# Loading the first layer's norm modulation by 2048-column rows, and 128-feature blocks for the first norm

## The chip, the cores and the metric

The kernel runs on one core of a Trainium2 chip. The metric is the device time of one launch in microseconds (us), lower is better. The engines are TensorE (PE; its weight loads are PEld), VectorE (DVE), ScalarE (ACT), GpSimd (POOL) and SyncE (SP), which here only issues DMAs. All arithmetic is float32.

## The reference

Two layers of a decoder trunk on x of 256 tokens by 1024 features. Each layer's two norms are modulated by a vector `mod` that is computed from a conditioning vector c.

```
c_act = silu(c)
for l in range(2):
    mod = c_act @ ada_w[l] + ada_b[l]          # (1, 6144): ada_w[l] is 1024 x 6144
    sh1, sc1, g1, sh2, sc2, g2 = split(mod, 6)
    h = rms_norm(x) * (1 + sc1) + sh1          # the first norm
    mix = mixing_sublayer(h, w_in[l], w_out[l], ...)   # h @ w_in[l] (1024 x 3584), attention, HGRN2
    x = x + g1 * mix
    h = rms_norm(x) * (1 + sc2) + sh2          # the second norm
    x = x + g2 * grouped_moe(h, w_router, w_gate[l], w_up[l], w_down[l])   # 16 experts, top 2
return rms_norm(x, final_norm)
```

## The kernel before, in words

**Weights.** Everything large streams from HBM in pieces of 1 MiB (a tile of 128 partitions by 2048 numbers) through a ring of slots. `Ring.specs` is the list of pieces in order of use; SP issues the next one (L97) when a slot is free, and `release` frees a slot once its matmuls are queued. The list begins with the eight pieces of ada_w that give sh1 and sc1 of layer 0 (blocks b = 0 to 3 of 512 columns, two pieces each), then w_in of layer 0 (HF, HQ, AQ, ..., with further ada_w pieces between), w_out, the experts of layer 0, and the same for layer 1. `spec8` cuts a block of 512 columns into two pieces by the view "(p j) f -> p j f": partition p holds rows 8p to 8p+7, four of them in a piece, in runs of 512 numbers (2 KB).

**Modulation of the first norm, layer 0** (`ada_cols`, called in `mixing`). For each block b, `ada_rows` multiplies the silu of c by the block: four matmuls side by side in 32-column strips of PE per piece (L323, output tile `at`), and DVE folds in the bias (L331, tile `acc`). `ada_col` turns the block of 512 results into columns by eight matmuls against a vector of ones (L358), which sum the four strips, and DVE copies 64 partitions of them into `mcol` (L360). `mcol[p, w, j]` holds shift (w = 0) and scale plus one (w = 1) of feature 8p + j.

**The first norm.** `mixing` scales x by 1/rms into `xh` (L435), transposes it by 16 PE transposes that each take every eighth feature, `xh[:, tt, j::8]` (L438), and ACT and DVE apply scale and shift in turns into `hx` (L483, L481). `hx[:, j, :]` then is the operand of the input projection: L492 for the blocks whose result has channels on partitions, L503 for those with tokens there. 1/rms comes from four squares on ACT (L409), a sum on DVE (L416) and two POOL instructions (L315, L316, the second a power). `lower_bounds` and `rope_tables` run in the same stretch: small parameters are transposed by PE (L271) from `prow`, and sine and cosine tables are made on ACT and DVE (`cosf`, L307) and copied by POOL (L516).

**Layer 1's modulation of the first norm** is made during the mixing of layer 0 (`ada_next`): DVE multiplies and adds the eight pieces (L346, tile `accn`), PE sums over partitions into one row (`row_to_col`, L364), ACT copies the row (L367), and a POOL DMA spreads it into columns of `mcol` (L368). The second norm's blocks go through `row_to_col` too.

**The order on an engine** is not that of the code: a scheduler of the build sorts the instructions of each engine by a simulated timeline. On the chip every engine then works through its own list in that order and waits at each instruction for what it needs. In the trace a float32 matmul shows as two MATMUL records, so four matmuls read x8.

Of the kernel before, what the change touches and what calls it, by code (L numbers as in the profile page):

```python
# [14 lines left out]
P = 128  # L15
# [107 lines left out]
def tile_trunk(ctx: ExitStack, tc: tile.TileContext, x, c, positions, w_in, w_out, attn_norm,  # L123
# [17 lines left out]

    def spec8(label, src):
        v = src.rearrange("(p j) f -> p j f", j=8)
        return [(label + (h,), 512, v[:, 4 * h:4 * h + 4, :]) for h in range(2)]
# [27 lines left out]
    for l in range(L):  # L172
        if l == 0:
            for b in range(4):
                add_ada(l, b)
        for b in (HF, HQ, AQ, AK, AV, HI, HG):
            ring.specs += spec8(("in", l, b), w_in[l, :, b * 512:(b + 1) * 512])
            for a in ADA_AFTER[b]:
                add_ada(l, a)
            if l + 1 < L:  # L180
                for a in COL_AFTER[b]:
                    add_ada(l + 1, a)
# [26 lines left out]
    early = lp.tile([P, 2048], F32, tag="s3", name="early")  # L209
    prow = early[0:32, 0:128]  # L210
    pcol = cp.tile([P, 24], F32, name="pcol")
    gp.memset(brow, 0.0)
# [10 lines left out]
    for i, w in enumerate((lb_params, attn_norm, hgrn_norm)):  # L223
        sy.dma_start(prow[8 * i:8 * i + 8, :], w.rearrange("l (g p) -> (l g) p", p=P))
    with nc.allow_non_contiguous_dma(reason="small parameter columns"):
        sy.dma_start(posi, positions[0].rearrange("(t p) -> p t", p=P))
# [42 lines left out]
    def lower_bounds():  # L269
        pst = psum("mm")  # L270
        pe.transpose(pst[:, 0:24], prow[0:24, :], ident[0:24, 0:24])  # L271
        ve.tensor_copy(pcol, pst[:, 0:24])
        tmp4, mx4 = early[:, 132:136], early[:, 136:140]
# [77 lines left out]

    def ada_col(b, acc, tag):
        pst = psum(tag)
        w, half = {0: 0, 1: 1, 3: 2, 4: 3}[b // 2], b % 2
        av = acc.rearrange("k (m e) -> k m e", e=8)
        hs = slice(64 * half, 64 * half + 64)
        for j in range(8):
            pe.matmul(pst[hs, j:j + 1], av[:, :, j], ones[:, 0:1], start=True, stop=True,  # L358
                      tile_position=(0, 64 * half))
        ve.tensor_copy(mcol[hs, w, :], pst[hs, 0:8])  # L360

    def row_to_col(acc, w, half, row):
# [5 lines left out]
        gp.dma_start(mcol[64 * half:64 * half + 64, w, :], row[0:1, :].rearrange("o (p j) -> o p j", j=8))  # L368

    def ada_cols(l):  # L370
        prev = None
        for b in range(4):
            acc = ada_rows(l, b, "at")
            if prev is not None:
                ada_col(*prev, "mm")
            prev = (b, acc)
        ada_col(*prev, "mm")

# [52 lines left out]
    def mixing(l, sp, carry, scaled):  # L431
        xh = mp.tile([P, 2, D], F32, tag="h", name=f"xh{l}")
        pss = [psum(t) for t in ("tr", "tr", "hg", "hg")]
        for tt in range(2):
            ve.tensor_scalar(xh[:, tt, :], X[:, tt, :], nrm[:, tt:tt + 1], None, op0=ALU.mult)  # L435
            for j in range(8):
                o = (j % 2) * 256 + tt * 128
                pe.transpose(pss[j // 2][:, o:o + 128], xh[:, tt, j::8], ident)  # L438
        if l == 0:
            rope_tables()  # L440
            lower_bounds()
            ada_cols(0)
        sh = [lp.tile([P, 2048], F32, tag=f"s{i}", name=f"s{i}_{l}") for i in range(SHARED)]
# [305 lines left out]
        def ada_next():  # L749
            for i, b in enumerate(ORDER):  # L750
                for a in COL_AFTER[b]:
                    while used[0] < 8 * i + 8:
                        yield
                    box = []
                    yield from ada_rows_ve(l + 1, a, box)
                    row_to_col(box[0], a // 2, a % 2, None)
                    yield
# [630 lines left out]
```

## Time and profile before

| | |
|---|---|
| Time, median of 3 runs | 918.64 us (917.01 to 919.52) |
| The profiled execution's own time | 916.64 us |
| Its span in the profile | 914.9 us |
| PE busy | 833.1 us (91%) |
| DVE, ACT, POOL busy | 358.1, 191.6, 93.3 us |
| DMA | 293.16 MB, mean 320 GB/s |

The table says how much each engine did in the whole, not where the time is lost. The span falls into mixing and experts of layer 0, and the same of layer 1; the changed lines run at the start of layer 0 (up to 40 us), here and there in the mixing of layer 0, and in the first norm of layer 1.

### The profile page before, as it was taken

The numbers are of one execution on the slowest core, as the hardware profiler recorded it, in microseconds if no ns is written. First come the engines' busy times: TensorE is split into PE (matmuls) and PEld (weight loads), VectorE is DVE, ScalarE is ACT, GpSimd is POOL, SyncE is SP. The second block draws the span as 40 slices with busy tenths as digits, with TensorE's granted clock in tenths as the row PEclk, the third lists the DMA queues.
The fourth block names the chain that finished last, engine by engine and source line by source line (L and its number), as shares of the span: only waits on it lengthen the run. The fifth ranks groups of instructions, "written<-read, shape, count | busy, mean of one in ns | idle before, by whom it ended". The sixth has DMA issues, their size and how long they took to land. (4 is left out here: it accounts for less than half of the span.)

```text
span 914.9 us, 11907 instructions
## 1 busy us (share of the span) xinstructions
PE 833.1 (91%) x4569; PEld 428.8 (47%) x4569; DVE 358.1 (39%) x814; ACT 191.6 (21%) x386; POOL 93.3 (10%) x123
## 2 busy tenths in 40 slices
PE   4899999999899998889968999999989999889995
PEld 1588744654543342233316896565444434234322
DVE  2335886353722150222223468861363133023013
ACT  2121232331611110010021222252152011001112
POOL 0211330022000000000101332011200000000001
PEclk9899999999999999999998999999999999999998
DMA  9996577668789899999997633689669989999992
GB/s 331 385 330 224 184 276 266 256 261 342 303 336 406 342 416 402 416 404 404 411 387 261 230 122 111 231 303 336 239 227 394 409 334 422 395 416 407 422 386 90
DMA packets 97971, 293.16 MB, mean 320 GB/s; under 512 B 5558, under 2 KB 7886, under 8 KB 81512
## 3 DMA queue, kind: packets, MB, share of 16 engines
q1 hardware_dynamic: 97368, 291.93, 84.2%
q8 instruction: 40, 0.66, 0.3%
q14 instruction: 35, 0.29, 0.1%
q10 hardware_dynamic: 144, 0.26, 0.1%
q0 software_dynamic: 384, 0.03, 0.0%
HBM read 291.13 MB, written 1.05 MB: 319 GB/s over the span
## 5 line engine op out<-in xcount | busy, mean ns | idle before, releaser
L1049 PE MATMUL mm<-w,hg 128*32 128x512 f32 (+1 forms) x736 | 156.4, 595 | 2.1 <-DMA w<-in_w_up_dram 1.5
L1049 PE MATMUL mm<-s,hg 128*32 128x512 f32 (+1 forms) x576 | 141.2, 595 | 5.0 <-DMA s<-in_w_up_dram 3.5
L1049 PE MATMUL hg<-w,aT 128*32 128x512 f32 (+3 forms) x408 | 97.5, 584 | 2.9 <-DMA w<-in_w_down_dram 1.6
L492 PE MATMUL mm<-hx,w 128*128 128x256 f32 x352 | 82.6, 390 | 0.9 <-ACT hx L483 0.9
L1049 PE MATMUL hg<-s,aT 128*32 128x512 f32 (+1 forms) x312 | 72.7, 615 | 3.7 <-ACT aT L1073 2.5
L1049 PEld LDWEIGHTS mm<-w,hg 128*32 128x32 f32 (+1 forms) x736 | 42.3, 115 | 70.8 <-issue 65.6
L1066 DVE TENSOR_TENSOR a<-a,mm 128x512 f32<-128x512 f32 x14 | 9.6, 688 | 164.1 <-PE mm L1049 164.1
L492 PEld LDWEIGHTS mm<-hx,w 128*128 128x128 f32 x352 | 67.2, 195 | 13.9 <-issue 3.1
L1049 PEld LDWEIGHTS mm<-s,hg 128*32 128x32 f32 (+1 forms) x576 | 38.2, 119 | 59.5 <-issue 47.9
L492 PE MATMUL tr<-hx,w 128*128 128x256 f32 x256 | 57.3, 380 | 0.0
L1084 DVE SCALAR_TENSOR_TENSOR u<-hg,cws,mod 128x512 f32<-128x512 f32 x27 | 20.3, 751 | 90.4 <-PE hg L1049 84.7
L346 DVE SCALAR_TENSOR_TENSOR accn<-w,cact,accn 128x512 f32<-128x512 f32 x64 | 51.9, 811 | 4.7 <-DMA w<-in_ada_w_dram 3.3
L492 PEld LDWEIGHTS tr<-hx,w 128*128 128x128 f32 x256 | 48.2, 190 | 9.3 <-issue 3.1
L323 PE MATMUL at<-w,cz 128*32 128x512 f32 x208 | 34.5, 723 | 19.3 <-DMA w<-in_ada_w_dram 9.9
L503 PE MATMUL mm<-w,hx 128*128 128x512 f32 x112 | 50.9, 597 | 0.2 <-ACT s L575 0.2
L1093 DVE TENSOR_TENSOR X<-X,at 128x512 f32<-128x512 f32 x54 | 35.0, 683 | 29.7 <-PE at L1092 29.5
L1049 PEld LDWEIGHTS hg<-w,aT 128*32 128x32 f32 (+1 forms) x408 | 27.0, 120 | 41.6 <-issue 33.6
L1092 PE MATMUL at<-yy,scat 128*128 128x512 f32 x104 | 34.9, 433 | 11.5 <-ACT yy L1085 11.5
L1085 ACT ACTIVATE yy<-u 128x512 fp32r<-128x512 f32 x26 | 16.4, 629 | 117.2 <-DVE u L1084 117.2
L1049 PE MATMUL mm<-QT,hg 128*32 128x512 f32 (+1 forms) x96 | 37.3, 594 | 2.8 <-DMA QT<-in_w_up_dram 2.8
L1092 PEld LDWEIGHTS at<-yy,scat 128*128 128x128 f32 x104 | 16.5, 188 | 38.7 <-ACT yy L1085 20.4
L503 PEld LDWEIGHTS mm<-w,hx 128*128 128x128 f32 x112 | 20.6, 190 | 24.6 <-issue 24.0
(302 smaller groups left out, 1078.1 us busy)
## 6 DMA issues: line engine op xcount, KB each, us to landing
w<-in_ada_w_dram SPq DMA_DIRECT2D x42, 1024.0 KB, 9.2
w<-in_w_gate_dram SPq DMA_DIRECT2D x38, 1024.0 KB, 13.7
w<-in_w_down_dram SPq DMA_DIRECT2D x38, 1024.0 KB, 11.8
s<-in_w_up_dram SPq DMA_DIRECT2D x31, 1024.0 KB, 18.6
w<-in_w_in_dram SPq DMA_DIRECT2D x26, 1024.0 KB, 8.9
s<-in_w_gate_dram SPq DMA_DIRECT2D x25, 1024.0 KB, 12.9
w<-in_w_up_dram SPq DMA_DIRECT2D x24, 1024.0 KB, 18.9
s<-in_w_down_dram SPq DMA_DIRECT2D x24, 1024.0 KB, 17.1
```

Of the source, the lines that this page charges most:

```text
L323: pe.matmul(ps[32 * t:32 * t + 32, :], cz[:, r * 4 + t, :], w[:, t, :], start=(r == 0), stop=(r == 1), tile_position=(0, 32 * t))
L346: ve.scalar_tensor_tensor(acc, w[:, t, :], cact[:, j:j + 1], acc, op0=ALU.mult, op1=ALU.add)
L492: pe.matmul(o, w[:, cc], hx[:, j, :], start=j == 0 and cg % 2 == 0, stop=j == 7 and cg % 2 == 1)
L503: pe.matmul(pss[tt], hx[:, j, tt * 128:(tt + 1) * 128], w, start=j == 0, stop=j == 7)
L1049: marks[0] = pe.matmul(ps[a:a + n, :], lhs[:, a:a + n], ws[i], start=first, stop=last, tile_position=(0, a) if n < 128 else None)
L1066: ve.tensor_tensor(a, a, pu, op=ALU.mult)
L1084: ve.scalar_tensor_tensor(u, ps, cws, modB[3][:, hf * 512:(hf + 1) * 512], op0=ALU.mult, op1=ALU.mult)
L1085: ac.activation(yy[:, 0, :], u, AF.Copy)
L1092: pe.matmul(ps, sc[:, tt * 128:(tt + 1) * 128], yy[:, i, :], start=(i == 0), stop=(i == 1))
L1093: ve.tensor_tensor(X[:, tt, ds_], X[:, tt, ds_], ps, op=ALU.add)
```

## The change

Layer 0's sh1 and sc1 are loaded as eight pieces of one row in eight: piece j holds, on partition p, row 8p + j with all 2048 columns in one run (8 KB). `ada_first` takes the pieces as they come, and the four matmuls of a piece now are the four column blocks, each in its own strip of PE, added up over the eight pieces in one PSUM tile. ACT copies that tile once (L363), four transposes turn it (L366), and one DVE instruction picks the four columns that hold results, adds the bias and writes all of `mcol` for w = 0, 1 (L368). The bias comes from a new small DMA of ada_b into `prow` (L225) and through the transpose that was there for other parameters, now of 40 rows. Feature j*128 + p stands on partition p now, so `xh` is transposed in blocks of 128 neighbouring features, and w_in is viewed as "(j p) f -> p j f" in both layers. Layer 1's blocks are summed and turned into columns by four matmuls with `accn` as the stationary operand (L374) and an ACT copy (L376), in place of the row and the POOL DMA.

```diff
-    def spec8(label, src):
-        v = src.rearrange("(p j) f -> p j f", j=8)
+    def spec8(label, src, perm="(p j) f -> p j f"):
+        v = src.rearrange(perm, j=8)
...
         if l == 0:
-            for b in range(4):
-                add_ada(l, b)
+            v = ada_w[l, :, 0:2048].rearrange("(p j) f -> p j f", j=8)
+            ring.specs += [(("ada4", j), 2048, v[:, j:j + 1, :]) for j in range(8)]
...
-            ring.specs += spec8(("in", l, b), w_in[l, :, b * 512:(b + 1) * 512])
+            ring.specs += spec8(("in", l, b), w_in[l, :, b * 512:(b + 1) * 512], "(j p) f -> p j f")
...
+    sy.dma_start(prow[24:40, :], ada_b[0, 0:2048].rearrange("(k p) -> k p", p=P))
...
-        pe.transpose(pst[:, 0:24], prow[0:24, :], ident[0:24, 0:24])
-        ve.tensor_copy(pcol, pst[:, 0:24])
+        pe.transpose(pst[:, 0:40], prow, ident[0:40, 0:40])
+        ve.tensor_copy(pcol, pst[:, 0:40])
+        ve.tensor_scalar(pcol[:, 32:40], pcol[:, 32:40], 1.0, None, op0=ALU.add)
...
+    def ada_first():
+        ps = psum("at")
         for j in range(8):
-            pe.matmul(pst[hs, j:j + 1], av[:, :, j], ones[:, 0:1], start=True, stop=True,
-                      tile_position=(0, 64 * half))
-        ve.tensor_copy(mcol[hs, w, :], pst[hs, 0:8])
+            key, w = ring.take(("ada4", j))
+            for b in range(4):
+                pe.matmul(ps[32 * b:32 * b + 32, :], cz[:, j, :], w[:, 0, b * 512:(b + 1) * 512], start=(j == 0),
+                          stop=(j == 7), tile_position=(0, 32 * b))
+            ring.release(key)
+        acc = mp.tile([P, 512], F32, tag="acc", name="acc4")
+        ac.activation(acc, ps, AF.Copy)
+        pst = psum("mm")
+        for c in range(4):
+            pe.transpose(pst[:, c * 128:(c + 1) * 128], acc[:, c * 128:(c + 1) * 128], ident)
+        cols = mcol.rearrange("p w j -> p (w j)")[:, 0:16].rearrange("p (b c) -> p c b", b=4)
+        ve.tensor_tensor(cols, pst.rearrange("p (c b e) -> p c b e", c=4, b=4)[:, :, :, 0],
+                         pcol[:, 24:40].rearrange("p (b c) -> p c b", b=4), op=ALU.add)
+
+    def ada_col(b, acc):
+        w, half = b // 2, b % 2
+        pst = psum("at")
+        for c in range(4):
+            pe.matmul(pst[:, c:c + 1], acc[:, c * 128:(c + 1) * 128], ones[:, 0:1], start=True, stop=True)
+        ac.activation(mcol[:, w, 4 * half:4 * half + 4], pst[:, 0:4], AF.Copy)
...
-                pe.transpose(pss[j // 2][:, o:o + 128], xh[:, tt, j::8], ident)
+                pe.transpose(pss[j // 2][:, o:o + 128], xh[:, tt, j * 128:(j + 1) * 128], ident)
...
-            ada_cols(0)
+            ada_first()
...
-                    row_to_col(box[0], a // 2, a % 2, None)
+                    ada_col(a, box[0])
```

**PE at the start of layer 0.** From the last transpose of the first half of the tokens on, before (`w_5`, `w_6`, `w_7` are the last three ada_w pieces, `w_8` the first of w_in, `at` the sums, `mm_278` and `mm_288` the columns of blocks 2 and 3):

```order
L438 MATMUL hg_149<-cs,xh_145 128x128 x2
L323 MATMUL at_238<-w_5_99,cz 32x512 x4
L438 MATMUL tr_146<-cs,xh_145 128x128 x2
L438 MATMUL tr_147<-cs,xh_145 128x128 x2
L438 MATMUL hg_148<-cs,xh_145 128x128 x2
L438 MATMUL hg_149<-cs,xh_145 128x128 x2
L323 MATMUL at_263<-w_6_101,cz 32x512 x4
L358 MATMUL mm_278<-cs,acc_2_251 64x1 x8
L323 MATMUL at_263<-w_7_103,cz 32x512 x4
L358 MATMUL mm_288<-cs,acc_3_276 64x1 x8
L492 MATMUL mm_320<-hx,w_8_201 128x256 x2
```

And now, from the matmuls of `w_5` on (`acc_249` is ACT's copy of the sums; of the transposes the four rows of the first half of the tokens are left out, which read like those of the second):

```order
L359 MATMUL at_198<-w_5_100,cz 32x512 x4
...
L445 MATMUL tr_147<-cs,xh_146 128x128 x2
L445 MATMUL tr_148<-cs,xh_146 128x128 x2
L445 MATMUL hg_149<-cs,xh_146 128x128 x2
L445 MATMUL hg_150<-cs,xh_146 128x128 x2
L359 MATMUL at_198<-w_6_102,cz 32x512 x4
L359 MATMUL at_198<-w_7_104,cz 32x512 x4
L366 MATMUL mm_251<-cs,acc_249 128x128 x4
L499 MATMUL mm_279<-hx,w_8_203 128x256 x2
```

The matmuls of `w_5` moved ahead of all transposes of `xh`, and the two groups of column matmuls gave way to one group of four transposes.

**POOL on the way to 1/rms.** Before (`nrm` is 1/rms, `s` the tile of the copied tables):

```order
L315 TENSOR_SCALAR nrm<-nrm 128x2
L516 COPY s_0_304<-sinf 128x256
L316 TENSOR_TENSOR nrm<-nrm,mhalf 128x2
L457 MEMSET s_0_299 64x4x256
L458 MEMSET s_0_299 64x4x256
L459 MEMSET QT 64x4x256
L460 MEMSET QT 64x4x256
L516 COPY s_0_304<-cosf 128x256
```

And now:

```order
L523 COPY s_0_263<-sinf 128x256
L317 ISA
L317 TENSOR_SCALAR nrm<-nrm 128x2
L523 COPY s_0_263<-cosf 128x256
L318 TENSOR_TENSOR nrm<-nrm,mhalf 128x2
L464 MEMSET s_0_258 64x4x256
```

The copy of the cosine table, which stood behind the power and four memsets, now stands ahead of the power that ends `nrm`.

**DVE in the mixing of layer 0**, where the first pieces for layer 1 (`accn`) meet the start of HGRN2 (`hg` its PSUM tiles). Before:

```order
L346 SCALAR_TENSOR_TENSOR accn_0_551<-w_18_364,cact,accn_0_551 128x512 x4
L346 SCALAR_TENSOR_TENSOR accn_0_551<-w_19_372,cact,accn_0_551 128x512 x3
L595 TENSOR_TENSOR s_0_300<-s_0_298,s_0_299 64x1024 x2
L346 SCALAR_TENSOR_TENSOR accn_0_551<-w_19_372,cact,accn_0_551 128x512
L606 TENSOR_TENSOR s_0_299<-s_0_299,s_0_298 64x4x128 x2
L602 TENSOR_TENSOR s_0_301<-cs,hg_443 128x8x128
```

And now:

```order
L348 SCALAR_TENSOR_TENSOR accn_0_510<-w_18_323,cact,accn_0_510 128x512 x4
L602 TENSOR_TENSOR s_0_259<-s_0_257,s_0_258 64x1024 x2
L348 SCALAR_TENSOR_TENSOR accn_0_510<-w_19_331,cact,accn_0_510 128x512
L613 TENSOR_TENSOR s_0_258<-s_0_258,s_0_257 64x4x128 x2
L348 SCALAR_TENSOR_TENSOR accn_0_510<-w_19_331,cact,accn_0_510 128x512 x3
L609 TENSOR_TENSOR s_0_260<-cs,hg_402 128x8x128
```

Three of the `accn` instructions moved from ahead of the start of HGRN2 to between its second and third step.

## Rows read from the trace of the kernel before

**Rows 1.** The page's DMA share in 40 slices of the span, in tenths

```profile
DMA  9996577668789899999997633689669989999992
```

**Rows 2.** PE's groups by line, 39.8 to 230 us: xcount | busy us, mean ns | idle before <-releasers

```profile
L492 PE MATMUL mm<-hx,w 128*128 128x256 f32 x192 | 46.3, 396 | 0.9 <-ACT hx L483 0.9
...
L618 PE MATMUL hg<-s,s 128*128 128x128 f32 x112 | 14.2, 276 | 1.0 <-DVE s L631 1.0
...
L503 PE MATMUL mm<-s,hx 128*128 128x512 f32 x16 | 7.1, 599 | 1.2 <-DMA s<-in_w_in_dram 1.2
...
L364 PE MATMUL at<-accn,cs 128*1 128x512 f32 x8 | 4.1, 590 | 0.0
...
L683 PE MATMUL at<-s,QT 128*128 128x128 f32 x16 | 3.6, 305 | 0.8 <-DVE mx L689 0.8
...
L600 PE MATMUL hg<-heads,s 128*128 128x2 f32 x16 | 1.8, 246 | 0.0
```

**Rows 3.** Timeline, x to xh: start us, us, engine, line, tiles [idle before <-releaser]

```profile
18.39 0.63 ACT L409 ACTIVATE junk<-X 128x512 f32<-128x512 f32 x1 [15.82 <-DMA X<-in_x_dram]
...
24.39 0.40 POOL L516 COPY s<-sinf 128x256 f32<-128x256 f32 x1 [1.00 <-ACT sinf L304]
...
24.75 0.70 POOL L316 TENSOR_TENSOR nrm<-nrm,mhalf 128x2 f32<-128x2 f32 x1
...
24.95 0.18 DVE L307 TENSOR_SCALAR cosf<-early 128x64 f32<-128x64 f32 x1
...
25.92 2.54 DVE L435 TENSOR_SCALAR xh<-X,nrm 128x1024 f32<-128x1024 f32 x2
```

**Rows 4.** Timeline, from xh to the first matmul of the input projection

```profile
27.07 1.12 PE L438 MATMUL tr<-cs,xh 128*128 128x128 f32 x4 [0.92 <-DVE xh L435]
...
28.97 1.94 PE L323 MATMUL at<-w,cz 128*32 128x512 f32 x8
...
30.84 0.71 PE L438 MATMUL tr<-cs,xh 128*128 128x128 f32 x4
...
31.93 1.07 PE L323 MATMUL at<-w,cz 128*32 128x512 f32 x8
...
32.93 2.08 PE L358 MATMUL mm<-cs,acc 128*64 128x1 f32 x16
...
34.94 1.06 PE L323 MATMUL at<-w,cz 128*32 128x512 f32 x8
...
36.07 0.75 DVE L331 SCALAR_TENSOR_TENSOR acc<-brow,cs,at 128x512 f32<-128x512 f32 x1 [0.87 <-PE at L323]
...
36.87 2.08 PE L358 MATMUL mm<-cs,acc 128*64 128x1 f32 x16 [0.87 <-DVE acc L331]
...
39.81 6.96 PE L492 MATMUL mm<-hx,w 128*128 128x256 f32 x20 [0.86 <-ACT hx L483]
```

**Rows 5.** Windows: stretch, us, busy us of PE, PEld, DVE, ACT, POOL, PEclk, DMA, GB/s

```profile
31.00:37.80 6.80, 5.93 (x48) 4.05 (x48) 1.63 (x3) 0.00 (x0) 0.00 (x0) 1.00 1.04 384
37.90:44.60 6.70, 5.84 (x20) 4.79 (x21) 2.08 (x5) 1.94 (x4) 0.00 (x0) 0.50 1.05 386
44.70:55.00 10.30, 10.30 (x51) 9.09 (x50) 0.00 (x0) 1.88 (x2) 0.00 (x0) 1.00 1.05 387
...
358.70:362.10 3.40, 1.86 (x13) 0.73 (x11) 0.69 (x1) 0.60 (x1) 0.00 (x0) 1.00 1.05 387
```

**Rows 6.** DMA packets of 40 to 56 us, and of 340 to 350 us

```profile
DMA packets 3111, 6.18 MB, mean 386 GB/s; under 512 B 95, under 2 KB 95, under 8 KB 3111
...
DMA packets 583, 4.25 MB, mean 425 GB/s; under 512 B 64, under 2 KB 64, under 8 KB 64
```

**Rows 7.** DMA issues of 18.3 to 18.6 us: size, us to landing

```profile
w<-in_ada_w_dram SPq DMA_DIRECT2D x1, 1024.0 KB, 10.9
```

**Rows 8.** Timeline: an ACT copy of a whole PSUM tile

```profile
64.83 0.60 ACT L400 ACTIVATE mod<-at 128x512 f32<-128x512 f32 x1 [7.49 <-PE at L399]
```

**Rows 9.** DMA share in 40 slices of 212 to 230 us

```profile
DMA  9999999999998930000077989999989999999999
```

More of the change, by code (lines that the diff above doesn't have):

```diff
@@ L209, in tile_trunk @@
     early = lp.tile([P, 2048], F32, tag="s3", name="early")
-    prow = early[0:32, 0:128]
-    pcol = cp.tile([P, 24], F32, name="pcol")
+    prow = early[0:40, 0:128]
+    pcol = cp.tile([P, 40], F32, name="pcol")
     gp.memset(brow, 0.0)
@@ L350, in ada_rows_ve @@
         out.append(acc)
[L352 to L356, printed above, removed]
-        for j in range(8):
-            pe.matmul(pst[hs, j:j + 1], av[:, :, j], ones[:, 0:1], start=True, stop=True,
-                      tile_position=(0, 64 * half))
-        ve.tensor_copy(mcol[hs, w, :], pst[hs, 0:8])
+    def ada_first():
+        ps = psum("at")
+        for j in range(8):
+            key, w = ring.take(("ada4", j))
[17 more added lines that the diff above has]
+        ac.activation(mcol[:, w, 4 * half:4 * half + 4], pst[:, 0:4], AF.Copy)
     def row_to_col(acc, w, half, row):
@@ L368, in row_to_col @@
         gp.dma_start(mcol[64 * half:64 * half + 64, w, :], row[0:1, :].rearrange("o (p j) -> o p j", j=8))
[L370 to L377, printed above, removed]
     def ada_block(l, b, route):
```

## Prediction

> **What bounds the kernel now.** The page comes first, and of it the DMA share by slices [rows 1]: it is full up to about 70 us, falls to 6 to 9 tenths up to 200 us, and is full through most of the experts. So the start might be bound by the loads, the mixing hardly, the experts partly. The groups of PE's matmuls in the mixing of layer 0 tell the second thing [rows 2]: over 190 us PE sat idle 0.9 + 1.0 + 1.2 + 0.8, that is 3.9 us, and every other group has nothing before it. From the first matmul of the input projection (39.81 us) to the end of the mixing PE is the bound, and whatever brings that first matmul forward brings the experts forward.
>
> What holds it back until 39.81 is read from two pieces of the timeline. The first [rows 3]: x lands at 18.39, ACT squares it, the scheduler has put table loads, sine and cosine between, and POOL's power ends at 25.45; DVE starts to scale x at 25.92. The second [rows 4]: from 27.07 PE works through transposes, the pieces of ada_w and the column matmuls one after another. Its idle time there is the 0.87 us for DVE's bias and the 0.86 us for the copy and the first piece of `hx`. The last piece of ada_w lands 10.9 us after its issue at about 18.4 [rows 7], at 29.3, but is multiplied at 34.94. It is PE's queue, not the load, that is late.
>
> The third thing is PE's clock [rows 5]: 1.00 (2.4 GHz) from 31.0 to 37.8, 0.50 (1.2 GHz) from 37.9 to 44.6, 1.00 again from 44.7. It had risen after PE had worked without a pause from 27.07; it fell after a stretch in which PE did one full group (1.06 us), column matmuls and two waits. So the projection ran its first 4.8 us at half speed and lost 2.4 us.
>
> **The change part by part.** Start of PE's work on `xh`. Runs of 8 KB move faster than runs of 2 KB: 425 against 386 GB/s [rows 6], for 1 MiB 2.47 against 2.72 us. Four pieces stand ahead of x, so x lands 1.0 us earlier. The ends: nothing gained if what tells the two windows apart is not the run length, 1.0 us if it is; I take the gain, since the windows differ in little else. Against it, POOL now copies the cosine table ahead of the power. The table is ready at 25.13 on the old clock, the copy takes 0.40 and the power 0.70, so `nrm` is done at about 26.3 in place of 25.45, plus 0.9. Net zero on `nrm`; DVE's other small work, which kept `xh` until 25.92, is shorter by two bias and two column instructions less one new, so `xh` starts 0.5 us earlier, and the transposes at 26.6. If the loads are no faster they start at 27.5.
>
> PE from there. Transposes of the first half 1.9 us, of the second 1.9 (still at the lower clock; at the upper 1.1): 30.4. The matmuls of `w_5`, 1.94 us between the two halves before, now run in the idle time ahead, since `w_5` lands by 24 (two pieces of 2.7 ahead of the last, at 29.3) and no transposes are ready. `w_6` and `w_7` at the upper clock, 1.07 + 1.06: 32.5. That takes for granted that 3.8 us of work without a pause raise the clock as before. Nothing says that the moment of the rise repeats to the microsecond; half a microsecond goes on top for it: 33.0.
>
> The tail. Before, from the end of `w_7` (36.0): bias on DVE, 2.08 us of column matmuls, copy, first `hx`, 39.81, in all 3.8 us. Now: ACT copies the tile, 0.60 [rows 8] and 0.1 to start; four transposes, which as eight records cost half of the sixteen of `xh`, 1.2 us; DVE's addition of 16 numbers a partition, 0.2 as the small DVE instructions of this stretch (0.18 in [rows 3]), and 0.1; then as before 0.86 less the copy's 0.2, 0.65. In all 2.85 us: the first matmul of the projection at 35.8 in place of 39.81, **4.0 us earlier**. By parts: 0.5 for `xh`, 1.9 for `w_5`, 2.0 for the columns of block 2, 1.0 for the tail, less about 0.9 because the second transposes run at the lower clock, and 0.5 for the rise.
>
> The clock after that. Between the end of `w_7` and the projection PE now has 2.85 us with 1.2 us of transposes in it, where it had 3.8 us with column matmuls of one moving column. It is followed by the projection without a gap. From 358.7 to 362.1 PE stood idle for 1.5 us between full matmuls, and the clock was 1.00 [rows 5]. I take it that the clock stays up: **2.4 us**. The ends are 0 (it falls as before) and 2.4; a fall that starts with the projection and lasts as long as the whole of the old one, 6.8 us, costs 3.4 and so 1.0 more than before.
>
> Layer 1's columns. Four times, two records of 0.59 us, in all 0.95 to 1.0 (8 records of L364 in 4.1 us) [rows 2], become eight with a full weight load and one moving column. The nearest is L600, 16 records in 1.8 us, 0.9 for eight. Zero, at most 0.3 each if the loads don't overlap; I add 0.2. The four POOL DMAs and the row copies that go were hidden under PE's work.
>
> At nothing: the transposes of neighbouring features (the same records; a reading order is not seen in any row), the 40-row transpose, the one DVE instruction and the one small DMA, hidden in waits of the first 18 us on x. The new view of w_in has the same 2 KB runs, farther apart; its first piece landed at some 33 (0.44 MiB of constants and itself, 3.9 us, behind the last of ada_w), 6 us before its use, which comes 4 us earlier. Uncovered, 10% more for a load costs 0.3 us a piece.
>
> Sum: 4.0 + 2.4 - 0.2 = 6.2 us. From the profiled execution's 916.64 that gives 910.4; the median of the runs is 2.0 above that execution, so 912.4 on the scale of the runs. The experts of layer 0 run partly at the pace of DMA, but their stream starts from PE's work: at 218 to 222 us the DMA engines stand still [rows 9], because slots, not the stream, were the limit. So the shift should reach the end.
>
> **The rivals.** *The clock falls again.* For it: it did so in nearly the same place, and PE waits twice. Against it: the waits are shorter and the matmuls between fuller. Then 4.0 - 1.0 - 0.2 = 2.8 earlier, or 4.0 if it loses no more than before: 914.6 to 915.8.
>
> *Transposes don't wake the clock.* If only the matmuls of pieces count, PE runs at the lower clock through `w_6` and `w_7` (3.9 us: 34.3), the tail adds 2.85 (37.2), and the clock falls once more for 6.8 us: 2.6 - 1.0 - 0.2 = 1.4 earlier, 917.2. The Trainium skill, TensorE: Matmul & The Clock Gate, Part 4, states that PE's transpose mode does not count as busy for the clock. By that rule this rival is the forecast; the trace speaks more against it than for it, since the clock rose at 31.0 after a stretch that was half transposes [rows 4, 5].
>
> *The loads get slower.* Each ada_w run now is 8 KB at a distance of 192 KiB from the next partition's; before, the same partition's runs followed at 24 KiB. If that took 30% more time per piece, 0.8 us, the last one would land at 29.3 + 8 x 0.8 = 35.7, and the projection start at 35.7 + 1.1 + 2.85 = 39.6: no gain, 918.4. Against it: the 8 KB runs of the experts are the fastest in the trace. The Trainium skill, DMA: Bandwidth & Descriptors, Latency and other measured facts, gives a fall from 207 to 164 GB/s where rows lie 2 MiB apart in place of 512 KiB; 192 KiB is below both, and no run here shows such a distance with 8 KB runs.
>
> *Slower: HGRN2's start is late on DVE.* Three `accn` instructions now stand between its second and third step. The third step feeds PE's L618 and, at the end of that chain, frees the slots for the last w_in pieces, for which PE already waits 1.2 us [rows 2]. Three instructions of 0.8 us are 2.4 us. Since the chain alternates between PE and DVE, a PE list that was sorted for a faster one could stall at several places. From 6.2 us of such stalls on it decides; at 9 the time is 921.4. Against it: PE's idle for DVE is 1.8 us in the whole mixing.
>
> **How the numbers follow.** The forecast (clock stays, 910.5 to 914.5) 0.53; the clock falls again 0.2; transposes don't count 0.08; slower loads, or a gain swallowed by the experts' stream, 0.11; slower 0.08. A measurement of this kernel can tell some 0.3%, 2.8 us. Faster takes the forecast, and of the second case all that is over 2.8, with its share: 0.53 + 0.2 + the better half of the third, 0.77; same 0.15; slower 0.08. The range of 8 in 10 leaves out the slower case and the top of the slow loads above, and a little below: 910.0 to 917.3. The likeliest's own is 910.5 to 914.5.
>
> **What would show it.** The first L499 between 35 and 36.5 us; `w_5` multiplied before the transposes; the x wait ending near 17.4; PEclk 1.00 through 37 to 45 us, and no more than 4.5 us of PE idle from there to the end of the mixing. It is wrong where the first L499 comes after 38, where PEclk shows 0.50 for the projection's start, or where PE waits for `hg` or `s` by more than 3 us in the mixing.

## The result and the profile after

The changed kernel takes 906.03 us (median of 4 runs, 905.32 to 907.78) where the kernel before takes 918.77 (4 runs, 917.01 to 919.52): ratio 0.9869, 95% interval 0.9855 to 0.9883, so 12.7 us faster where 6.2 were forecast. The profiled execution of after is the longest of its four, 907.78 us with a span of 905.9; that of before, 916.64 us, lies below all four of its timed runs. Between the two profiles the gain is therefore only 8.9 us.

The timeline of after from x to `xh` answers to [rows 3]; columns as there.

```profile
17.43 0.63 ACT L416 ACTIVATE junk<-X 128x512 f32<-128x512 f32 x1 [14.86 <-DMA X<-in_x_dram]
...
23.42 0.39 POOL L523 COPY s<-sinf 128x256 f32<-128x256 f32 x1 [21.64 <-ACT sinf L306]
23.91 0.19 POOL L317 TENSOR_SCALAR nrm<-nrm 128x2 f32<-128x2 f32 x1
24.21 0.40 POOL L523 COPY s<-cosf 128x256 f32<-128x256 f32 x1
24.57 0.70 POOL L318 TENSOR_TENSOR nrm<-nrm,mhalf 128x2 f32<-128x2 f32 x1
...
25.31 2.96 DVE L442 TENSOR_SCALAR xh<-X,nrm 128x1024 f32<-128x1024 f32 x2 [1.09 <-POOL nrm L318]
```

x comes 0.96 us earlier (17.43 for 18.39). POOL's cosine copy stands ahead of the power, as the order said, and takes back part of that; `xh` starts 0.61 us earlier.

The same view from `xh` to the projection, on PE, ACT and DVE, answers to [rows 4].

```profile
22.51 1.93 PE L359 MATMUL at<-w,cz 128*32 128x512 f32 x8 [0.52 <-DMA w<-in_ada_w_dram]
...
26.89 1.11 PE L445 MATMUL tr<-cs,xh 128*128 128x128 f32 x4 [2.45 <-DVE xh L442]
...
29.50 0.91 PE L445 MATMUL hg<-cs,xh 128*128 128x128 f32 x4
30.34 1.92 PE L359 MATMUL at<-w,cz 128*32 128x512 f32 x16
...
32.33 0.60 ACT L363 ACTIVATE acc<-at 128x512 f32<-128x512 f32 x1 [8.83 <-PE at L359]
32.98 0.66 PE L366 MATMUL mm<-cs,acc 128*128 128x128 f32 x4 [0.72 <-ACT acc L363]
33.68 0.18 DVE L368 TENSOR_TENSOR mcol<-mm,pcol 128x16 f32<-128x16 f32 x1 [5.41 <-PE mm L366]
33.90 1.02 ACT L490 ACTIVATE hx<-tr,mcol 128x256 f32<-128x256 f32 x2 [0.97 <-DVE mcol L368]
34.51 0.70 PE L499 MATMUL mm<-hx,w 128*128 128x256 f32 x2 [0.87 <-ACT hx L490]
```

`w_5` is multiplied at 22.51, ahead of the transposes; these run without a pause, `w_6` and `w_7` follow as one group, and the projection starts at 34.51 in place of 39.81. The windows with the granted clock answer to [rows 5].

```profile
26.90:30.10 3.20, 3.20 (x15) 3.20 (x16) 1.37 (x1) 0.00 (x0) 3.09 (x3) 0.50 0.98 339
30.20:31.00 0.80, 0.80 (x10) 0.29 (x12) 0.00 (x0) 0.00 (x0) 0.00 (x0) 1.00 1.05 407
31.00:37.80 6.80, 5.21 (x31) 3.48 (x24) 2.09 (x5) 2.52 (x5) 0.00 (x0) 1.00 1.05 409
37.90:44.60 6.70, 6.70 (x35) 5.90 (x34) 0.00 (x0) 1.88 (x2) 0.00 (x0) 1.00 1.05 405
```

The clock stays at 1.00 through the projection's start, where before it was 0.50 from 37.9 to 44.6. Then one thing that no step spoke of: the last column, 405 to 409 GB/s where before showed 384 to 387. The DMA lines of after for 40 to 56 us (against [rows 6]) and for the experts, 250 to 450 us:

```profile
DMA packets 3287, 6.54 MB, mean 408 GB/s; under 512 B 96, under 2 KB 96, under 8 KB 3287
...
DMA packets 21741, 81.63 MB, mean 408 GB/s; under 512 B 1248, under 2 KB 1248, under 8 KB 15299
```

In 40 to 56 us the sizes are as before (nearly all 2 KB), the engines are as full, yet 3287 packets pass for 3111. In the experts the kernel before has this line:

```profile
DMA packets 19903, 77.99 MB, mean 390 GB/s; under 512 B 1176, under 2 KB 1176, under 8 KB 13464
```

The step from 390 to 408 is not all due to the packets. The experts of layer 0 begin at 247.59 us in before and at 240.12 in after, so the window holds another part of them. The changed kernel with its slots at another place (`after_unpad`, below), whose experts begin at 239.28, moves 400 GB/s in the same window:

```profile
DMA packets 20984, 79.90 MB, mean 400 GB/s; under 512 B 1213, under 2 KB 1213, under 8 KB 14582
```

So more than half of the step goes with where the window falls, and 8 of the 18 GB/s are left for the packets. Their records in the trace show it directly: in the first 60 us a 2 KB packet takes a median of 84 ns, before 87; in the experts an 8 KB packet 309, before 312.

The stages in one table, from one profile each; every border is the start of a group on PE (first projection matmul, first router transpose of X, first expert matmul), worked out from the instruction records. The kernels of the rows from `before_pad` on come below.

| | start | mixing 0 | router 0 | experts 0 | mixing 1 | router 1 | experts 1 | span |
|---|---|---|---|---|---|---|---|---|
| before | 39.81 | 190.29 | 17.49 | 242.57 | 172.49 | 16.04 | 236.16 | 914.85 |
| after | 34.51 | 188.12 | 17.49 | 241.19 | 172.48 | 16.04 | 236.08 | 905.91 |
| before_pad | 39.19 | 189.86 | 17.49 | 241.97 | 172.49 | 16.02 | 233.68 | 910.69 |
| after_256 | 34.62 | 188.04 | 17.51 | 241.62 | 172.48 | 16.04 | 233.91 | 904.21 |
| l1row | 35.46 | 188.06 | 16.10 | 241.12 | 172.47 | 16.05 | 235.58 | 904.83 |
| after_unpad | 35.58 | 187.66 | 16.03 | 244.23 | 172.48 | 16.03 | 237.09 | 909.11 |
| after_128 | 35.42 | 187.87 | 16.03 | 244.16 | 172.49 | 16.04 | 236.27 | 908.28 |
| before_warm | 40.20 | 189.39 | 17.50 | 242.83 | 172.48 | 16.05 | 238.49 | 916.94 |
| xfirst | 32.03 | 190.59 | 16.04 | 236.12 | 171.52 | 16.04 | 235.37 | 897.72 |
| xfirst_warm | 35.29 | 188.18 | 16.03 | 239.89 | 172.49 | 17.50 | 234.11 | 903.49 |

A router stage is 16.0 or 17.5, as the clock does or does not fall there; this differs between executions of one kernel (router 1 of before takes 16.04 here and 17.49 in two more profiles of it). It and the experts' stage move single spans by a few us, so sizes below are taken from ratios of medians, and the table only says where. Each ratio is to runs of the kernel before on the same chip; the experiments ran on several chips, so their medians alone don't compare to a microsecond.

### The profile page after: what moved, and what is told of

It reads as the page before. It is cut to its first block, busy times and chain, and to the rows that moved or that the text cites. A ratio compares the mean times of both kernels' runs of the same rounds, so it can differ in the third digit from the quotient of the medians.

```text
span 905.9 us, 11822 instructions
## 1 busy us (share of the span) xinstructions
PE 824.9 (91%) x4533; PEld 423.6 (47%) x4533; DVE 354.0 (39%) x808; ACT 190.4 (21%) x387; POOL 91.1 (10%) x119
## 5 line engine op out<-in xcount | busy, mean ns | idle before, releaser
L499 PE MATMUL mm<-hx,w 128*128 128x256 f32 x352 | 80.3, 382 | 0.9 <-ACT hx L490 0.9
L1056 PEld LDWEIGHTS hg<-w,aT 128*32 128x32 f32 (+1 forms) x408 | 26.2, 120 | 43.8 <-issue 35.8
L1099 PE MATMUL at<-yy,scat 128*128 128x512 f32 x104 | 35.0, 434 | 11.5 <-ACT yy L1092 11.5
L1099 PEld LDWEIGHTS at<-yy,scat 128*128 128x128 f32 x104 | 16.5, 188 | 38.8 <-ACT yy L1092 20.5
L638 DVE TENSOR_TENSOR s<-s,s 64x256 f32<-64x256 f32 x56 | 31.5, 562 | 0.7
```

The costliest lines, as they stand in the source:

```text
L499: pe.matmul(o, w[:, cc], hx[:, j, :], start=j == 0 and cg % 2 == 0, stop=j == 7 and cg % 2 == 1)
L638: ve.tensor_tensor(qv[:, :, :, 1, :], qv[:, :, :, 1, :], tv[p0:p1, :, :, 0:1].to_broadcast([p1 - p0, 4, nb, h]), op=ALU.mult)
L1056: marks[0] = pe.matmul(ps[a:a + n, :], lhs[:, a:a + n], ws[i], start=first, stop=last, tile_position=(0, a) if n < 128 else None)
L1099: pe.matmul(ps, sc[:, tt * 128:(tt + 1) * 128], yy[:, i, :], start=(i == 0), stop=(i == 1))
```

## The experiments

The theories after the first comparison. One: the change's own steps (earlier start, clock kept) gave it all, and the faster packets are one execution's luck or come of the 8 KB runs. Two: `pcol` grew by 16 columns of 4 bytes, and with it every tile allocated behind it, the slots of all the large loads, moved by 64 bytes; packets are faster for where they land.

**Is the packet time one execution's?** `before_b1` and `before_b2` are the kernel before again, `after_a1` the changed kernel, no line changed.

> The kernel before once more, to see how far its executions differ and where. Theory A (the 8.9 us between the two profiles are the change, the remaining 3.8 us between the medians are scatter of single executions): time 917 to 920, first matmul of the projection between 39 and 41.5 us, its length from there to the experts' end within 1 us of the profile before, and what is over it lies in the stretches where the clock is low or in the experts. Rival B (the profile before was an outlier at its start): first matmul of the projection at 42 us or later, 2 us or more behind the profile before.

> The same kernel, a third profile. Theory A: as in the run ahead of it, 917 to 920, the first matmul of the projection at 39 to 41.5. Rival B: at 42 or later.

> The changed kernel once more. Theory A (all of the gain is made ahead of the end of the first projected block: the earlier first matmul, 5.3 us, and the clock that stays up, 2.4 us; what is over 7.7 us is scatter): ratio to before 0.986 to 0.991, first matmul of the projection at 34 to 35.5 us, clock 1.00 through the first 10 us of it. Theory B (part of the gain is made in the experts of layer 0, whose loads meet free slots earlier): the experts of layer 0 take 241.2 us again, 1.4 less than in the profile before and than in the two other profiles of before.

Measured: 919.10 and 919.75 us, one time each; `after_a1` 908.43 (6 runs), ratio 0.9876 (0.9856 to 0.9897). The start is at 39.78 and 40.44 in before, at 34.21 in after; mixing 0 takes 190.5 and 190.2 against 187.8. So the first profile of before was no outlier at its start. Theory B is borne out too: the experts of layer 0 take 241.48 us in `after_a1`, against 243.01 and 243.25. The first copy of before moves 386 GB/s at 40 to 50 us, as the first profile did:

```profile
DMA packets 1945, 3.86 MB, mean 386 GB/s; under 512 B 62, under 2 KB 62, under 8 KB 1945
```

The packet time belongs to the program: the median of 2 KB packets in the first 60 us is 86 to 87 ns in all three profiles of before and 84 in both of after.

**Is it the 8 KB runs?** `runs2k` keeps the changed kernel, but loads each of the first eight pieces as two DMAs with 2 KB runs.

```diff
-            self.parts.append([(v[:, :, a:b], src[:, :, a:b]) for a, b in cuts])
+            if label[0] == "ada4":
+                q = "p o (x y f) -> p (o y) x f"
+                dv, sv = v.rearrange(q, x=2, y=2), src.rearrange(q, x=2, y=2)
+                self.parts.append([(dv[:, y], sv[:, y]) for y in range(2)])
+            else:
+                self.parts.append([(v[:, :, a:b], src[:, :, a:b]) for a, b in cuts])
```

> The changed kernel with each of the first eight pieces loaded by two DMAs whose runs are 2 KB in place of 8 KB; nothing else differs. If the longer runs brought x forward by 1.0 us and that goes through to the projection: x is used at 18.3 in place of 17.4, the projection starts at 35.3 to 35.6, and the time is 0.8 to 1.2 us more than the changed kernel's (ratio to before 0.987 to 0.989). If the run length is hidden behind the small instructions on ACT, POOL and DVE: the projection starts at 34.5 and the time is the changed kernel's.

Measured: 908.26 us (5 runs), ratio 0.9871 (0.9851 to 0.9891), no difference from the changed kernel. x is used at 18.13 and the projection starts at 35.67, where PE waits 1.56 us for the first piece of w_in. So the long runs bring x 0.7 us forward (18.13 to 17.43), but the 0.8 to 1.2 us that were expected at the end do not show. At 40 to 50 us it still moves 407 GB/s: the later loads' speed does not come of the runs.

**Is it the place?** Three kernels change nothing but the room that `pcol` takes. `before_pad` gives the kernel before the changed kernel's room; `after_unpad` and `after_128` move the changed kernel's slots to other places.

```diff
 before_pad
-    pcol = cp.tile([P, 24], F32, name="pcol")
+    pcol = cp.tile([P, 40], F32, name="pcol")[:, 0:24]
 after_unpad
-    pcol = cp.tile([P, 40], F32, name="pcol")
+    pcol = cp.tile([P, 88], F32, name="pcol")[:, 0:40]
 after_128
-    pcol = cp.tile([P, 40], F32, name="pcol")
+    pcol = cp.tile([P, 72], F32, name="pcol")[:, 0:40]
```

> The kernel before with nothing but a longer tile: pcol takes 40 columns in place of 24 as in the change, which moves every tile behind it by 64 bytes a partition, the ring's slots from 64 past a multiple of 128 bytes to a multiple of 512. No instruction differs. Theory C (the place of the slots sets the time of a DMA packet, and through it 1.5 to 3 us of the change's gain): packets of 2 KB take 84 ns in the median from 20 to 55 us in place of 88, the experts of layer 0 take 241.3 us in place of 242.6 to 243.3, and the time is 2 to 3.5 us less than before's. Rival D (the packets are faster for another reason: which rows a piece holds, the view of w_in): packets stay at 88 ns and the time is before's within 0.5 us.

> The changed kernel with pcol at 88 columns: the slots stand 64 bytes past a multiple of 128 again, as before the change; no instruction differs. Theory C: packets of 2 KB take 88 ns, of 8 KB 315; the experts of layer 0 take 242.5 to 243.5 us; the time is 1.5 to 3.5 us more than the changed kernel's 908.4 (ratio to before 0.989 to 0.991). Rival D: 84 and 310 ns, and the changed kernel's time.

> The changed kernel with pcol at 72 columns: slots at a multiple of 128 bytes, but not of 256 or 512. Theory C with a step of 128 bytes or less: packets of 84 ns and the changed kernel's time. If it takes a multiple of 256 or 512: 88 ns, and the time of the run with the slots 64 bytes off.

Later `after_256` (a room of 104 columns) was added, to tell which multiple it takes.

> The changed kernel, pcol's room 104 columns in place of 40, so that every tile behind it starts 256 bytes past a multiple of 512 (in the changed kernel on a multiple of 512, in the kernel before 448 past it); no instruction differs. If a multiple of 256 bytes is enough for a load's destination: packets of 2 KB 84 ns, time 906 +- 1.5, as the changed kernel. If it takes a multiple of 512: 88 ns and 910 to 911, as with the room of 88 and of 72 columns. If the place of the tiles is not the cause at all, nothing ties the packets to the room, and 88 or 84 may come here with any time.

The DMA lines at 40 to 50 us, first `before_pad`:

```profile
DMA packets 2056, 4.08 MB, mean 408 GB/s; under 512 B 64, under 2 KB 64, under 8 KB 2056
...
q1 hardware_dynamic: 2056, 4.08, 105.0%
```

then `after_unpad`:

```profile
DMA packets 1950, 3.86 MB, mean 386 GB/s; under 512 B 63, under 2 KB 63, under 8 KB 1950
...
q1 hardware_dynamic: 1950, 3.86, 104.9%
```

The engines are equally busy in both (last figure, share of 16 engines), and the packets that pass differ by 5%. With the bytes by which the slots' start lies past a multiple of 512, from the addresses of the built programs:

| kernel | bytes past 512 | GB/s at 40 to 50 us | median, us | ratio (interval) |
|---|---|---|---|---|
| before | 448 | 386 | 918.65 | 1 |
| before_pad | 0 | 408 | 914.81 | 0.9960 (0.9944 to 0.9976) |
| after | 0 | 409 | 906.03 | 0.9869 (0.9855 to 0.9883) |
| after_256 | 256 | 408 | 905.74 | 0.9868 (0.9849 to 0.9887) |
| after_unpad | 192 | 386 | 910.90 | 0.9909 (0.9893 to 0.9925) |
| after_128 | 128 | 387 | 910.07 | 0.9924 (0.9897 to 0.9950) |

No instruction differs between before and `before_pad`, nor among the four kernels with the change. The place moves both kernels by 0.4 to 0.55%, 3.7 to 5 us, and of the places tried the two on a multiple of 256 bytes (0 and 256) are fast; 128, 192 and 448 are not. The Trainium skill, DMA: Bandwidth & Descriptors, How a descriptor splits into AXI transactions, says that the first transaction of a descriptor which doesn't start on a multiple of 256 bytes starts at the boundary below it, and that the bytes fetched ahead of the start are unused and still cost beats, the 32-byte steps of the transfer. These runs agree in where the border lies; the page puts it for the reading side of a transfer, and here it is the place that is written. That this is the mechanism here is not shown.

Not every number came as expected. `before_pad` gains 3.8 us between the medians, where 2 to 3.5 were expected; the experts of layer 0 take 241.97 there in place of 241.3, and 244.2 in `after_unpad` and `after_128` in place of 242.5 to 243.5. For the changed kernel the table of stages says where the place costs: `l1row` (below; slots as in after) and `after_unpad` start within 0.12 us of each other and both keep the clock up in router 0, and the experts of layer 0 then take 241.12 and 244.23, three microseconds more at the worse place. For the kernel before the profiles do not tell where: `before_pad` is shorter mainly in the experts of layer 1 (233.68 for 236.16), but after and `after_256`, both at a good place, differ there by as much.

**Layer 1's columns.** `l1row` takes them back to the row matmul with DMAs on POOL's queue.

```diff
+    def row_to_cols(b, acc):
+        w, half = b // 2, b % 2
+        ps = psum("at")
+        pe.matmul(ps[0:1, :], ones[:, 0:1], acc, start=True, stop=True)
+        row = mp.tile([P, 512], F32, tag="acc", name="row")
+        ac.activation(row[0:1, :], ps[0:1, :], AF.Copy)
+        for j in range(4):
+            gp.dma_start(mcol[:, w, 4 * half + j:4 * half + j + 1],
+                         row[0:1, 128 * j:128 * j + 128].rearrange("o (p e) -> o p e", e=1))
...
-                    ada_col(a, box[0])
+                    row_to_cols(a, box[0])
```

> The changed kernel with layer 1's blocks summed into a row by one matmul again and spread by POOL DMAs (four a block, of single numbers, since the layout is the new one). The prediction's term: 0.2 us to the better, hidden otherwise, so the time is that of the changed kernel within 0.5 us. Rival: the rows on ACT and the DMAs that POOL waits for held the mixing up; then the mixing of layer 0 takes 1 us or more over the 188 of the changed kernel.

Measured: 906.80 us (4 runs), ratio 0.9869 (0.9851 to 0.9887), that of the change. The group in the mixing of layer 0 is, in after,

```profile
L375 PE MATMUL at<-cs,accn 128*128 128x1 f32 x32 | 3.9, 243 | 0.0
```

against 4.1 us before [rows 2]. This part is worth nothing that can be measured, either way (the interval is 1.7 us to either side).

**The clock alone.** `before_warm` is the kernel before with matmuls that nobody reads: two of 128x256 in the wait for the last bias, two in that for the last column copy.

```diff
+            if (l, b, r) == (0, 3, 1):
+                warm = psum(tag)
+                for n in range(2):
+                    pe.matmul(warm[:, 0:256], w[:, 0, 0:128], w[:, n, 0:256], start=True, stop=True)
             ring.release(key)
...
+        warm = psum("at")
+        for n in range(2):
+            pe.matmul(warm[:, 0:256], acc[:, 0:128], acc[:, 0:256], start=True, stop=True)
```

> The kernel before with four matmuls of 128x256 whose result nobody reads, two in the wait for the last bias and two in the wait for the last column copy, just ahead of the projection; nothing else differs. If the fall of the clock there cost 2.4 us and came of PE's thin work: granted clock 1.00 from 31 to 45 us, first matmul of the projection at 39.8 to 40.3, mixing 187.7 to 188.2 in place of 190.3, 916 to 917 (ratio 0.9975). If the clock falls anyway at that time, or costs nothing: 918 to 919.5 (ratio 1.000).

Its PE row at that place, and its windows:

```profile
35.17 1.07 PE L323 MATMUL at<-w,cz 128*32 128x512 f32 x8
36.16 1.13 PE L328 MATMUL at<-w 128*128 128x256 f32 x4
37.22 2.08 PE L362 MATMUL mm<-cs,acc 128*64 128x1 f32 x16
39.23 1.13 PE L384 MATMUL at<-acc 128*128 128x256 f32 x4
40.20 2.17 PE L499 MATMUL mm<-hx,w 128*128 128x256 f32 x9
```

```profile
31.00:37.80 6.80, 6.80 (x53) 4.54 (x49) 1.65 (x3) 0.00 (x0) 0.00 (x1) 1.00 1.05 386
37.90:44.60 6.70, 6.70 (x37) 5.92 (x37) 2.08 (x5) 1.94 (x4) 0.00 (x0) 1.00 1.05 387
...
157.20:160.60 3.40, 3.18 (x4) 1.51 (x5) 0.39 (x2) 0.59 (x1) 0.52 (x1) 0.50 1.05 406
```

Measured: 915.92 us (12 runs, 914.02 to 920.29), ratio 0.9982 (0.9967 to 0.9998): 1.7 us (0.2 to 3.0). The pauses are filled and the clock doesn't fall at 37.9; the projection starts 0.4 us later and still the kernel gains. Mixing 0 took 189.39 in the profiled execution, not the 187.7 to 188.2 expected: the clock fell once within it, in 157.2 to 160.6 us, which before did not show. By an estimate half of those 3.4 us, 1.7, is lost, and without it mixing 0 would be near 187.7, as in the changed kernel. The gain is that of the prediction's 2.4 us less the 0.4 of the later start, within its wide interval.

**What holds the start now.** `xfirst` is the changed kernel with x and the small parameters issued ahead of the pieces of ada_w; `xfirst_warm` adds matmuls that nobody reads behind the pieces.

```diff
 xfirst
+    sy.dma_start(X, x[0].rearrange("(t p) d -> p t d", p=P))
...
-    ring.gate = 2
-    ring.pump()
...
-    ring.gate = 4
...
-    sy.dma_start(X, x[0].rearrange("(t p) d -> p t d", p=P))
...
+    ring.gate = 2
...
+    ring.gate = 4
+    ring.pump()
 xfirst_warm, beyond that
+        warm = psum("at")
         for j in range(8):
...
+            if j >= 2:
+                for n in range(2 if j == 7 else 4):
+                    pe.matmul(warm[:, 0:256], w[:, 0, 0:128], w[:, 0, n * 256:(n + 1) * 256], start=True, stop=True)
```

> The changed kernel with the loads of x and of the small parameters issued ahead of the eight pieces of ada_w. x is then no longer late: the transposes of xh stand ahead of the second piece in PE's row, and the last landing of ada_w (some 27.5 us) sets the end: first matmul of the projection at 31 to 32.5 us in place of 34.5. Theory that PE's clock depends on what PE did just before: PE now works in short groups with pauses while it waits for the pieces, the clock is at 0.50 when the projection starts, and its mixing takes 190 us or more in place of 188.1: 905 to 906 in all, most of the gain is lost. Rival, that the clock rises from work of any density: mixing 188, 903 to 904.

> As the run with x first, and behind the pieces 2 to 7 of ada_w four (behind the last one two) matmuls of 128x256 whose result nobody reads, so that PE's pauses between the pieces are filled. If the clock is what the run with x first lacks: granted clock 1.00 before the projection starts, which it does at 31.5 to 33, mixing 187.5 to 188.2, 903 to 904, the fastest of all. If the clock rises there without them: equal to the run with x first or up to 1 us slower. If the experts' loads set their end whatever the start: 905.5 to 906.5.

PE's timeline in `xfirst`, and its windows:

```profile
11.97 1.11 PE L445 MATMUL tr<-cs,xh 128*128 128x128 f32 x4 [0.39 <-DVE xh L442]
...
26.93 1.07 PE L359 MATMUL at<-w,cz 128*32 128x512 f32 x8 [0.90 <-DMA w<-in_ada_w_dram]
28.72 0.66 PE L366 MATMUL mm<-cs,acc 128*128 128x128 f32 x4 [0.72 <-ACT acc L363]
32.03 1.34 PE L499 MATMUL mm<-hx,w 128*128 128x256 f32 x3 [2.65 <-DMA w<-in_w_in_dram]
```

```profile
24.00:32.00 8.00, 3.26 (x22) 0.78 (x21) 1.95 (x5) 2.53 (x5) 0.00 (x0) 0.91 0.99 370
32.10:35.70 3.60, 3.60 (x9) 2.88 (x10) 0.05 (x1) 0.00 (x0) 0.00 (x0) 0.53 1.07 412
35.70:50.00 14.30, 14.30 (x77) 11.09 (x75) 1.92 (x6) 3.08 (x4) 0.00 (x0) 1.00 1.05 406
```

And the same windows in `xfirst_warm`:

```profile
24.00:32.00 8.00, 8.00 (x48) 4.78 (x48) 0.00 (x0) 0.00 (x0) 0.00 (x0) 1.00 1.01 379
32.10:35.70 3.60, 2.73 (x18) 1.56 (x11) 0.61 (x2) 1.62 (x4) 0.00 (x0) 1.00 1.05 408
```

`xfirst`: 899.70 us (4 runs), ratio 0.9807 (0.9787 to 0.9826), the fastest version here, about 6 us under the changed kernel. The start is 2.5 us earlier and the bound has moved: `hx` is ready, and PE waits 2.65 us for the first piece of w_in. PE was busy 3.26 of the 8 us ahead of that, the clock was at 0.53 for the next 3.6, and mixing 0 takes 190.59 in place of 188.12: 2.5 lost, as the theory of the clock said (by an estimate the 3.4 us at the lower clock make 1.7 of them). So nothing is left of the earlier start at the end of mixing 0: it is at 222.62 us, in after at 222.63. But the total is 5 to 6 us under the 905 to 906 that this theory gave. The table puts those in router 0 (1.45, the clock's fall that comes and goes), experts 0 (5.1) and mixing 1 (1.0). The waits of PE from 238 to 482 us show what sped the experts up (us in total, times, longest), first after, then `xfirst`:

```profile
PE at L1099 <- ACT yy L1092: 6.5, 6, 1.5
```

```profile
PE at L1099 <- ACT yy L1092: 1.5, 1, 1.5
```

L1099 is the matmul that scatters an expert's result to its tokens; it waits for ACT's copy of that result (`yy`). The build's scheduler put these matmuls elsewhere in PE's list in `xfirst`; this wait is 5.0 us shorter and the stage 5.1. So the fastest version seems to owe most of its gain over the changed kernel to an order of PE's instructions in the experts, not to x coming first; no run has that order alone.

`xfirst_warm`: 904.89 us (4 runs), ratio 0.9856 (0.9836 to 0.9876); it was expected to be the fastest and is not. The clock is at 1.00 through the start and mixing 0, which takes 188.18, as expected. But four such matmuls take 1.99 us, more than the pauses they were to fill, and the projection starts at 35.29. The largest difference to `xfirst` is again in experts 0, 239.89 against 236.12: here PE waits 6.2 us in six times for ACT's copies, as in after.

## Why the prediction was wrong: a term that it did not have, and the terms that it had

**The step that failed** is the list "at nothing", with the 40-row transpose and the wider `pcol` that takes it. The instructions there are indeed hidden, but the tile's 64 bytes were priced not at all. They put every slot behind it on a multiple of 256 bytes. `before_pad` measures this alone, 0.4% (3.7 us, 2.2 to 5.1), and `after_unpad` takes back as much from the change. The sum had no term for packets, and [rows 6] could not have told of it, since the kernel before has one place only. Without the shift the change is worth 0.9% (0.9909, 8.4 us by the ratio), with an interval of 6.9 to 9.8 us: the 6.2 lies just below it. `after_128`, also at a worse place, gives 7.0 us (4.6 to 9.5), which holds it. Of the 2.2 us between 6.2 and 8.4 the tail gives 0.5 and layer 1's columns 0.2 (below); the rest is not tied to a term.

**The first matmul of the projection, 4.0 us earlier.** It is 5.3 earlier in the profile of after, and part of that is luck with the clock. In after it rose at 30.1, ahead of `w_6`; in `after_unpad` it rose at 32.1, `w_6` and `w_7` took 2.59 us in place of 1.92, and the projection started at 35.58, 4.2 earlier:

```profile
30.73 2.59 PE L359 MATMUL at<-w,cz 128*32 128x512 f32 x16
```

That this comes of the place of the slots is not shown: `l1row` has them where after has them, yet its clock rose at 32.4 and its projection started at 35.46. With an early rise (after, `after_a1`, `after_256`) the start is 34.21 to 34.62, with a late one (`l1row`, `after_unpad`, `after_128`) 35.42 to 35.58; 35.8 was forecast. By parts, in after:
- `xh` 0.5 earlier: 0.61. POOL's copy ahead of the power took back most of what x brought: the power ends at 25.27 for 25.45, where no change was forecast. x came 0.96 earlier, of which `runs2k` gives 0.7 to the runs; the rest stays open, since three profiles of the kernel before differ by 0.65 in when x is used (18.13 to 18.78).
- `w_5` ahead of the transposes, block 2's columns gone: as forecast; `w_7` ends at 32.26 (30.34 + 1.92). The half microsecond for the moment of the clock's rise was not needed in this execution; in the three with the late rise it was.
- The tail of 2.85 us measured 2.25 (32.26 to 34.51). The four transposes took 0.66, not 1.2: a transpose is one record, not two, as the order rows ahead of the prediction already had it (x4), where "eight records" was assumed. This term was 0.5 us too large.

**The clock, 2.4 us.** Right: 1.00 through 37.9 to 44.6, mixing 0 shorter by 2.2 to 2.6, and `before_warm` gives the term its own run: 1.7 us (0.2 to 3.0) with a start 0.4 us later.

**Layer 1's columns, -0.2.** Not to be told from zero, by `l1row`; 0.2 us is less than its interval can tell.

**"The shift should reach the end."** Mostly. In `after_unpad` the router of layer 0 is 1.46 us shorter by a clock that stayed up, and its experts are 1.66 longer than those of before. That the experts partly run at the pace of their loads fits this and the three microseconds between `l1row` and `after_unpad` there.

**From profile to median, 2.0 us.** Added to the forecast since before's profiled execution was short. After's was long by 1.75, so the difference between the two profiles (8.9) understates that of the medians (12.7). One execution of each bears no correction of that size.

**The rivals.** The clock did not fall again at the projection. Transposes did wake the clock: PE stood idle for 2.45 us up to 26.89, and from there to the rise at 30.1 it did nothing but the transposes of `xh`. The Trainium skill, TensorE: Matmul & The Clock Gate, Part 4, says that they don't count; this trace speaks against it. The loads did not get slower with the distance of 192 KiB: PE waited 0.52 us for `w_5`, ahead of the transposes, and not at all for `w_6` and `w_7`, and 8 KB packets take a median of 309 ns up to 60 us as they do in the experts. HGRN2 did not start late: the group of its chain in mixing 0 still waits 1.0 us for DVE, as in [rows 2]:

```profile
L625 PE MATMUL hg<-s,s 128*128 128x128 f32 x112 | 14.0, 276 | 1.0 <-DVE s L638 1.0
```

## What to carry to other kernels

When an edit changes a tile's size, look at where everything allocated behind it ends up: here 64 bytes in a tile of parameters were worth as much as most of the steps that were costed, and one kernel with only the size changed (`before_pad`) tells the two apart. Where PE stands in short waits just ahead of a long run of matmuls, read the granted clock of the run's first microseconds; filling the waits can pay (`before_warm`), filling more than the waits doesn't (`xfirst_warm`). And after a start has been shortened, see which wait ends last there now: with x first it was the first piece of w_in, not the work that had been moved. Read the other stages too before the gain is put down to the edit: that of `xfirst` lay in the experts, where the build had ordered PE's instructions otherwise.

## What the runs showed of the hardware

The time of a DMA packet goes with the SBUF address that it is written to: with nothing but the place of the tiles changed, 2 KB packets took a median of 84 ns (first 60 us) with the slots on multiples of 256 bytes, and 86 to 88 ns at 128, 192 and 448 past a multiple of 512; 8 KB packets 309 and 312 ns in the experts. The loss is 2 to 4 ns a packet in both sizes, a larger share of the short one. Not explained: the 4 KB packets of x took 159 ns in after, `before_pad` and `after_unpad`, and 164 before, though x's tile is allocated ahead of `pcol` and has the same address in all; and the 8 KB packets of the first pieces took 309 ns in `after_unpad` too.

The granted clock of PE rose from 0.50 to 1.00 in a stretch in which PE did nothing but 128x128 float32 transposes for 3.2 us (after, 26.89 to 30.1). The moment of that rise differed by 2.4 us between two profiles with the same instructions (29.8 in `after_a1`, 32.1 in `after_unpad`).
